# A rotary embedding kernel: the fp32 tail of the last row waits for another store and leaves in four DMAs

## The chip, the cores and the metric

The kernel runs on one core of a Trainium2 chip. The metric is the device time of one execution in microseconds (us), the median of several executions.

## The reference

The kernel computes an interleaved rotary position embedding on an fp32 tensor `x` of shape (8, 2048, 16, 64): batch, sequence, heads, head dimension. Neighbouring elements of the head dimension form a pair, which is rotated by an angle that depends on the position in the sequence and on the pair.

```
x1, x2 = x_pairs[..., 0], x_pairs[..., 1]
out1 = x1 * cos - x2 * sin
out2 = x1 * sin + x2 * cos
out = np.stack([out1, out2], axis=-1).reshape(batch, seq_len, num_heads, head_dim)
```

`cos` and `sin` have shape (2048, 32). The output is fp32 and as large as the input, 67.1 MB each.

## The kernel before, in words

The 2048 positions of a batch row are laid over 128 partitions, K = 16 positions to a partition, so a batch row is a tile of 128 x 16 x 1024 elements. In SBUF rows are held in bf16: `rows_sb` has NX = 5 slots of one batch row each, and row b lies in slot b % 5. Rows 5, 6 and 7 thus use the slots 0, 1 and 2 again.

Loads and stores of whole rows are DMAs that GpSimd (POOL) issues, and they convert between fp32 in HBM and bf16 in SBUF on the way (`load` at lines 51 to 56, `store` at lines 58 to 63; lines 56 and 63 move two rows in one DMA). Two pieces go in fp32 through a staging tile `st` instead, issued by SyncE (SP): the first HEAD = 4 positions of row 0, which ScalarE (ACT) then casts to bf16 (line 99), and the last TAIL = 4 positions of row 7, which ScalarE casts to fp32 (line 131) ahead of their store (line 132).

`rotate` (lines 79, 80 and 85) is three VectorE operations on a row in place: multiply by the signed sine table into `qt`, multiply by the cosine table, and add the pair-swapped `qt`.

The order is written out by hand. Rows 0 to 4 are loaded at the start, the stores of rows 0 and 1 are held back until the loads have landed (lines 111 and 112), and rows 5 to 7 are loaded once the slots are free. At the end the order on POOL is: the store of rows 3 and 4, of rows 5 and 6, and of the first twelve positions of row 7 (`store(7, k1=K - TAIL)`). Line 130 copies a single element of row 7 over an element of slot 4. Its result is used by nobody: as an instruction that writes to slot 4, it has to wait until the DMA that reads slot 4, the store of rows 3 and 4, has landed, and until row 7 is rotated. The cast at line 131 follows on the same engine, and the DMA at line 132 follows the cast. At line 158 the program ends: SP waits for all DMAs, the engines drain and meet.

Of the kernel before, what the change touches and what calls it, by code (L numbers as in the profile page):

```python
# [2 lines left out]

# [4 lines left out]


@with_exitstack  # L10
def kernel(
    ctx: ExitStack,
    tc: tile.TileContext,
    x: bass.AP,
    cos: bass.AP,
    sin: bass.AP,
    out: bass.AP,
):
    nc = tc.nc
    fp32 = mybir.dt.float32  # L20
    bf16 = mybir.dt.bfloat16
    mult = mybir.AluOpType.mult
    add = mybir.AluOpType.add

    B, S, H, D = x.shape
    P = 128
    K = S // P
    D2 = D // 2
    HD = H * D
    NX = 5  # L30
    HEAD = 4
    TAIL = 4
    REST = 2

    x_t = x.rearrange("b (p k) h d -> p b k (h d)", p=P, k=K)
    out_t = out.rearrange("b (p k) h d -> p b k (h d)", p=P, k=K)
    cos_t = cos.rearrange("(p k) c -> p (k c)", p=P, k=K)
    sin_t = sin.rearrange("(p k) c -> p (k c)", p=P, k=K)

    consts = ctx.enter_context(tc.tile_pool(name="consts", bufs=1))  # L40
    stage = ctx.enter_context(tc.tile_pool(name="stage", bufs=1))

    cos_sb = consts.tile([P, K * D2], fp32)
    sin_sb = consts.tile([P, K * D2], fp32)
    c_tab = consts.tile([P, K, D], bf16)
    s_tab = consts.tile([P, K, D], bf16)
    mark = consts.tile([1, 1], bf16)

    rows_sb = consts.tile([P, NX, K, HD], bf16)

    def load(b, n=1, k0=0, k1=K):
        s = b % NX
        if n == 1:
            nc.gpsimd.dma_start(out=rows_sb[:, s, k0:k1], in_=x_t[:, b, k0:k1])  # L54
        else:
            nc.gpsimd.dma_start(out=rows_sb[:, s : s + n], in_=x_t[:, b : b + n])  # L56

    def store(b, n=1, k1=K):
        s = b % NX
        if n == 1:  # L60
            nc.gpsimd.dma_start(out=out_t[:, b, :k1], in_=rows_sb[:, s, :k1])  # L61
        else:
            nc.gpsimd.dma_start(out=out_t[:, b : b + n], in_=rows_sb[:, s : s + n])  # L63

    def rotate(b, k0=0, k1=K):

        nk = k1 - k0
        xp = rows_sb[:, b % NX, k0:k1]
        qt = stage.tile([P, K, HD], bf16, name="qt", tag="work")

        def rows(a):
            return a.rearrange("p k (h e) -> p k h e", h=H, e=D)

        def tab(a):
            return dataclasses.replace(
                a, offset=a.offset + k0 * D, ap=[a.ap[0], [D, nk], [0, H], [1, D]]
            )

        nc.vector.tensor_tensor(out=rows(qt[:, :nk]), in0=rows(xp), in1=tab(s_tab), op=mult)  # L79
        nc.vector.tensor_tensor(out=rows(xp), in0=rows(xp), in1=tab(c_tab), op=mult)  # L80
        q_swap = dataclasses.replace(
            qt, offset=qt.offset + 1, ap=[qt.ap[0], [2, nk * HD // 2], [-1, 2]]
        )
        x3 = xp.rearrange("p k (a j) -> p (k a) j", j=2)
        nc.vector.tensor_tensor(out=x3, in0=x3, in1=q_swap, op=add)  # L85
        return qt

    with tc.manual_schedule():
        head = stage.tile([P, HEAD, HD], fp32, name="st", tag="work")
        nc.sync.dma_start(out=head, in_=x_t[:, 0, :HEAD])  # L90
        load(0, k0=HEAD)
        nc.gpsimd.dma_start(out=cos_sb, in_=cos_t)  # L92
        nc.gpsimd.dma_start(out=sin_sb, in_=sin_t)  # L93
        load(1, 2)
        load(3)
        load(4, k1=K - REST)
        load(4, k0=K - REST)

        nc.scalar.copy(out=rows_sb[:, 0, :HEAD], in_=head)  # L99
        s2 = s_tab.rearrange("p k (i j) -> p (k i) j", j=2)  # L100
        nc.vector.tensor_copy(out=s2[:, :, 0], in_=sin_sb)  # L101
        nc.vector.tensor_scalar_mul(s2[:, :, 1], sin_sb, -1.0)  # L102
        nc.vector.tensor_copy(  # L103
            out=c_tab.rearrange("p k (i j) -> p (k i) j", j=2),
            in_=cos_sb.to_broadcast([P, K * D2, 2]),
        )
        rotate(0, 0, HEAD)
        rotate(0, HEAD, K)
        rotate(1)

        nc.scalar.copy(out=mark, in_=rows_sb[:1, 4, K - REST - 1, :1])  # L111
        nc.scalar.copy(out=rows_sb[:1, 0, 0, :1], in_=rows_sb[:1, 0, 0, :1])  # L112
        store(0, 2)
        rotate(2)
        store(2)
        load(5, 2)
        load(7)
        rotate(3)
        rotate(4)
        store(3, 2)  # L120
        rotate(5)
        rotate(6)
        store(5, 2)
        rotate(7)
        store(7, k1=K - TAIL)


        tail = stage.tile([P, TAIL, HD], fp32, name="st", tag="work")
        last = rows_sb[:, 7 % NX]
        nc.scalar.copy(out=rows_sb[:1, 4, 0, :1], in_=last[:1, K - 1, :1])  # L130
        nc.scalar.copy(out=tail, in_=last[:, K - TAIL :])  # L131
        nc.sync.dma_start(out=out_t[:, B - 1, K - TAIL :], in_=tail)


# [1 line left out]
_INS = ['x', 'cos', 'sin']  # L136
_OUTS = [((8, 2048, 16, 64), 'float32')]


# [23 lines left out]
```

## Time and profile before

| | |
|---|---|
| median of 3 executions | 316.97 us (316.95 to 317.14) |
| the profiled execution | 317.52 us |
| its span in the profile | 315.7 us |
| VectorE busy | 210.3 us, 67% of the span |
| ScalarE, GpSimd busy | 8.9 us each, 3% |
| HBM read, written | 67.63 MB, 67.11 MB |

Times in the profile count from the start of the span. A line such as L132 is a line of the kernel. POOL is GpSimd, SP is SyncE, DVE is VectorE, ACT is ScalarE; a `q` behind a name is the sequencer of that engine. A DMA's time to landing runs from its issue to the semaphore that tells of its end. Each DMA engine of the core moves packets from two queues: q0 holds the DMAs that POOL issued, q1 those that SP issued. The profiled execution is one run, slightly longer than the median.

### The profile page before, as it was taken

How to read it: one execution, taken by the hardware profiler on the slowest of the kernel's cores; microseconds unless marked ns; L12 is line 12 of the kernel's file. 1: busy time of each engine (PE TensorE's matmuls, PEld its weight loads, DVE VectorE, ACT ScalarE, POOL GpSimd, SP SyncE). 2: the span in 40 equal slices, each digit the busy share in tenths (PEclk: the TensorE clock that was granted, in tenths of full speed). 3: DMA queues.
4: the chain of work that ended last, by engine and by line, in shares of the span. 5: the costliest groups of instructions: out<-in, count | busy, mean ns of one | idle time of the engine just before them, and what ended most of it. 6: DMA issues, size and time to landing. Idle time of an engine off the chain costs nothing.

```text
span 315.7 us, 117 instructions
## 1 busy us (share of the span) xinstructions
DVE 210.3 (67%) x30; ACT 8.9 (3%) x6; POOL 8.9 (3%) x18
## 2 busy tenths in 40 slices
DVE  0009995099999999999992000899999999900000
ACT  1030000000000000000000000000000000040000
POOL 5000000000000000000000000000000000000000
DMA  8999999999999999999999999999999999999997
GB/s 260 254 282 199 199 199 266 199 199 220 220 232 257 399 531 399 399 498 432 399 199 253 212 199 199 266 199 332 440 490 399 399 506 423 399 399 465 459 372 299
DMA packets 2816, 102.24 MB, mean 324 GB/s; under 512 B 256, under 2 KB 256, under 8 KB 512
## 3 DMA queue, kind: packets, MB, share of 16 engines
q0 software_dynamic: 2528, 98.04, 96.6%
q1 hardware_dynamic: 288, 4.19, 5.7%
HBM read 67.63 MB, written 67.11 MB: 427 GB/s over the span
## 4 chain that ended last, share of the span: by engine, by line
DVE 66%; another core or an unknown queue 13%; ACTq 1%; issue 0%; ACT 0%; DVEq 0%
DVE rows_sb L80 22%; DVE rows_sb L85 22%; DVE qt L79 22%; ACTq L158 1%; DVE c_tab L103 0%; ACT rows_sb L130 0%; DVEq L79 0%; DVEq L80 0%
## 5 line engine op out<-in xcount | busy, mean ns | idle before, releaser
L79 DVE TENSOR_TENSOR qt<-rows_sb,s_tab 128x16384 bf16<-128x16384 bf16 (+2 forms) x9 | 69.7, 7743 | 42.0 <-DMA rows_sb<-in_x_dram 41.8
L80 DVE TENSOR_TENSOR rows_sb<-rows_sb,c_tab 128x16384 bf16<-128x16384 bf16 (+2 forms) x9 | 69.7, 7743 | 0.4
L85 DVE TENSOR_TENSOR rows_sb<-rows_sb,qt 128x16384 bf16<-128x16384 bf16 (+2 forms) x9 | 69.7, 7744 | 0.3
L101 DVE CAST s_tab<-sin_sb 128x512 bf16<-128x512 f32 x1 | 0.5, 454 | 23.8 <-DMA sin_sb<-in_sin_dram 23.8
L63 POOL DMA_DIRECT2D out_dram<-rows_sb x3 | 2.2, 719 | 184.0 <-ACT rows_sb L112 94.3
L130 ACT COPY rows_sb<-rows_sb 1x1 bf16<-1x1 bf16 x1 | 0.2, 194 | 177.5 <-DVE rows_sb L85 177.5
L99 ACT CAST rows_sb<-st 128x4096 bf16<-128x4096 f32 x1 | 3.6, 3604 | 13.2 <-DMA st<-in_x_dram 13.2
L131 ACT CAST st<-rows_sb 128x4096 f32<-128x4096 bf16 x1 | 3.6, 3598 | 0.0
L54 POOL DMA_DIRECT2D rows_sb<-in_x_dram x5 | 2.9, 605 | 19.1 <-DMA out_dram<-rows_sb 18.3
L111 ACT COPY mark<-rows_sb 1x1 bf16<-1x1 bf16 x1 | 0.2, 193 | 80.3 <-DMA rows_sb<-in_x_dram 80.3
L61 POOL DMA_DIRECT2D out_dram<-rows_sb x2 | 1.1, 556 | 40.4 <-DVE rows_sb L85 40.4
L56 POOL DMA_DIRECT2D rows_sb<-in_x_dram x2 | 1.5, 728 | 25.0 <-DMA out_dram<-rows_sb 25.0
L99 ACT ACT_TABLE_LOAD x1 | 1.3, 1283 | 0.7 <-PEq L147 0.7
L103 DVE CAST c_tab<-cos_sb 128x1024 bf16<-128x1024 f32 x1 | 0.7, 685 | 0.0
L93 POOL DMA_DIRECT2D sin_sb<-in_sin_dram x1 | 0.6, 562 | 0.0
L92 POOL DMA_DIRECT2D cos_sb<-in_cos_dram x1 | 0.6, 554 | 0.0
L102 DVE TENSOR_SCALAR s_tab<-sin_sb 128x512 bf16<-128x512 f32 x1 | 0.4, 444 | 0.0
L112 ACT COPY rows_sb<-rows_sb 1x1 bf16<-1x1 bf16 x1 | 0.2, 188 | 0.0
L147 POOL MEMSET const-float32-0.0<- 128x1 f32 x1 | 0.1, 99 | 0.2 <-issue 0.2
L147 POOL MEMSET const-bfloat16-1.0<- 128x1 bf16 x1 | 0.1, 103 | 0.0
L147 POOL MEMSET const-float32-1.0<- 128x1 f32 x1 | 0.1, 99 | 0.0
L147 POOL MEMSET const-uint8-127<- 128x1 uint8 x1 | 0.1, 99 | 0.0
## 6 DMA issues: line engine op xcount, KB each, us to landing
rows_sb<-in_x_dram POOLq DMA_DIRECT2D x2, 8192.0 KB, 58.5
rows_sb<-in_x_dram POOLq DMA_DIRECT2D x2, 4096.0 KB, 68.0
out_dram<-rows_sb POOLq DMA_DIRECT2D x1, 6144.0 KB, 37.3
rows_sb<-in_x_dram POOLq DMA_DIRECT2D x1, 3584.0 KB, 94.8
rows_sb<-in_x_dram POOLq DMA_DIRECT2D x1, 3072.0 KB, 21.2
st<-in_x_dram SPq DMA_DIRECT2D x1, 2048.0 KB, 14.4
out_dram<-st SPq DMA_DIRECT2D x1, 2048.0 KB, 33.7
rows_sb<-in_x_dram POOLq DMA_DIRECT2D x1, 512.0 KB, 96.8
```

The source lines that it names most:

```text
L54: nc.gpsimd.dma_start(out=rows_sb[:, s, k0:k1], in_=x_t[:, b, k0:k1])
L56: nc.gpsimd.dma_start(out=rows_sb[:, s : s + n], in_=x_t[:, b : b + n])
L61: nc.gpsimd.dma_start(out=out_t[:, b, :k1], in_=rows_sb[:, s, :k1])
L63: nc.gpsimd.dma_start(out=out_t[:, b : b + n], in_=rows_sb[:, s : s + n])
L79: nc.vector.tensor_tensor(out=rows(qt[:, :nk]), in0=rows(xp), in1=tab(s_tab), op=mult)
L80: nc.vector.tensor_tensor(out=rows(xp), in0=rows(xp), in1=tab(c_tab), op=mult)
L85: nc.vector.tensor_tensor(out=x3, in0=x3, in1=q_swap, op=add)
L92: nc.gpsimd.dma_start(out=cos_sb, in_=cos_t)
L99: nc.scalar.copy(out=rows_sb[:, 0, :HEAD], in_=head)
L103: nc.vector.tensor_copy(out=c_tab.rearrange("p k (i j) -> p (k i) j", j=2), in_=cos_sb.to_broadcast([P, K * D2, 2]),)
L131: nc.scalar.copy(out=tail, in_=last[:, K - TAIL :])
L158: with _tile.TileContext(nc) as tc:
```

## The change

Line 130 writes its element to slot 6 % 5 = 1 instead of slot 4. Slot 1 is read by the store of rows 5 and 6. The tail, one DMA of four positions before, becomes four DMAs on SP: the first three positions of all 128 partitions, and the last position of partitions 0 to 111, 112 to 119 and 120 to 127.

```diff
         last = rows_sb[:, 7 % NX]
-        nc.scalar.copy(out=rows_sb[:1, 4, 0, :1], in_=last[:1, K - 1, :1])
+        nc.scalar.copy(out=rows_sb[:1, 6 % NX, 0, :1], in_=last[:1, K - 1, :1])
         nc.scalar.copy(out=tail, in_=last[:, K - TAIL :])
-        nc.sync.dma_start(out=out_t[:, B - 1, K - TAIL :], in_=tail)
+        nc.sync.dma_start(out=out_t[:, B - 1, K - TAIL : K - 1], in_=tail[:, : TAIL - 1])
+
+        for p0, p1 in ((0, P - 16), (P - 16, P - 8), (P - 8, P)):
+            nc.sync.dma_start(out=out_t[p0:p1, B - 1, K - 1], in_=tail[p0:p1, TAIL - 1])
```

## The prediction

> **What bounds the kernel now.** I read the page first: the shares of the engines, the strip of the DMA, the packets.
>
> ```profile
> span 315.7 us, 117 instructions
> DVE 210.3 (67%) x30; ACT 8.9 (3%) x6; POOL 8.9 (3%) x18
> DMA  8999999999999999999999999999999999999997
> DMA packets 2816, 102.24 MB, mean 324 GB/s; under 512 B 256, under 2 KB 256, under 8 KB 512
> q1 hardware_dynamic: 288, 4.19, 5.7%
> HBM read 67.63 MB, written 67.11 MB: 427 GB/s over the span
> ```
>
> VectorE, the busiest engine, works 67% of the span, while the DMA strip has a 9 in every slice but the first and the last. The 134.7 MB that cross HBM go at 427 GB/s over the whole span, the start and the end included. So the kernel is bound by its DMA engines, and an instruction matters only where it lets them run empty, or after their last byte. The packet row also shows how a DMA ends: the program issues 16 DMAs (9 loads and the head, 5 stores and the tail), and 256 packets are under 512 B, which is 16 for each. The row of q1 agrees: head and tail, 2 x 128 rows of 16 KB, are 256 packets, and 32 are left. So each of these DMAs is spread over 16 DMA engines and ends with a small packet on each.
>
> Then the timeline, for the stores and the end of the kernel.
>
> ```profile
> 99.68 0.72 POOL L63 DMA_DIRECT2D out_dram<-rows_sb  x1 [94.30 <-ACT rows_sb L112]
> 115.36 0.57 POOL L61 DMA_DIRECT2D out_dram<-rows_sb  x1 [14.96 <-DVE rows_sb L85]
> 250.95 0.72 POOL L63 DMA_DIRECT2D out_dram<-rows_sb  x1 [82.44 <-DVE rows_sb L85]
> 268.13 8.69 DVE L85 TENSOR_TENSOR rows_sb<-rows_sb,qt 128x16384 bf16<-128x16384 bf16 x1
> 276.86 0.19 ACT L130 COPY rows_sb<-rows_sb 1x1 bf16<-1x1 bf16 x1 [177.48 <-DVE rows_sb L85]
> 276.96 3.60 ACT L131 CAST st<-rows_sb 128x4096 f32<-128x4096 bf16 x1
> 277.13 0.54 POOL L61 DMA_DIRECT2D out_dram<-rows_sb  x1 [25.46 <-DVE rows_sb L85]
> 280.58 0.35 SPq L132 DMA_DIRECT2D out_dram<-st  x1
> ```
>
> The DMA view, asked for the stretch around each of these issues, gives the time from issue to landing; these are the answers for the issues at 99.68, 115.36, 250.95, 277.13 and 280.58.
>
> ```profile
> out_dram<-rows_sb POOLq DMA_DIRECT2D x1, 40.7
> out_dram<-rows_sb POOLq DMA_DIRECT2D x1, 44.3
> out_dram<-rows_sb POOLq DMA_DIRECT2D x1, 46.4
> out_dram<-rows_sb POOLq DMA_DIRECT2D x1, 6144.0 KB, 37.3
> out_dram<-st SPq DMA_DIRECT2D x1, 2048.0 KB, 33.7
> ```
>
> The landings are 99.68 + 40.7 = 140.38 (rows 0 and 1), 115.36 + 44.3 = 159.66 (row 2), 250.95 + 46.4 = 297.35 (rows 5 and 6), 277.13 + 37.3 = 314.43 (twelve positions of row 7) and 280.58 + 33.7 = 314.28 (the tail). Row 2 alone, 8.389 MB in fp32, landed 19.28 us after the store before it: 435 GB/s, which I take as the full rate. By its line, the wait on the store of rows 3 and 4 ended at 256.3:
>
> ```profile
> L130 ACTq EVENT_SEMAPHORE  x1: 38/38/38, 256.3 to 256.3; - x1
> ```
>
> From there to 314.43 the rows 5 and 6, row 7 and the tail go out, 24 MiB or 25.17 MB in 58.13 us, 433 GB/s. At 435.1 it would be 57.85 us: the whole end of the kernel has about 0.28 us to spare. VectorE finishes at 276.8 and the queue has 37.6 us of bytes left then.
>
> **The change part by part.** *The tie.* Line 130 now writes into slot 1, which the store of rows 5 and 6 still reads. ScalarE waits for that landing instead of for VectorE's last addition. Behind it in ScalarE's queue stands only the cast of the tail, and behind that SP's DMAs; POOL, whose last store is issued at 277.13, waits for none of them. With the tail no longer among its packets, rows 5 and 6 (16.78 MB at 435.1 GB/s, 38.56 us) land at 256.3 + 38.56 = 294.9. Copy and cast take 276.96 - 276.86 + 3.60 = 3.70 us, so SP issues at 298.6 instead of 280.58: 18 us later. What hides this is the rest of the store of row 7: 6.291 MB at 435.1 GB/s, 14.46 us from 294.9 on, to 309.3. SP's four issues at 0.35 us end at 300.0, over 9 us before the queue would run empty. The bytes are the same 8.389 MB behind 294.9, and at 435.1 GB/s they end at 314.2, or at 314.4 with the same slack as now. Cost 0. Only the order changes: row 7 first, the tail last and alone. If this cover were gone, the price would be the gap itself, microsecond for microsecond.
>
> *Three more DMAs on one queue.* Each adds its ending packets behind its bytes. The nearest rows are two small loads, one right behind the other, in POOL's queue:
>
> ```profile
> 1.93 0.55 POOL L92 DMA_DIRECT2D cos_sb<-in_cos_dram  x1
> 2.47 0.56 POOL L93 DMA_DIRECT2D sin_sb<-in_sin_dram  x1
> cos_sb<-in_cos_dram POOLq DMA_DIRECT2D x1, 256.0 KB, 21.2
> sin_sb<-in_sin_dram POOLq DMA_DIRECT2D x1, 256.0 KB, 21.3
> ```
>
> They land at 23.13 and 23.77, 0.64 us apart; 262,144 bytes at 435.1 GB/s are 0.60, so the second DMA cost 0.04 us beyond its bytes, although its pieces are small. Stores may cost more: the 0.28 us of slack in the last 58.13 us holds three changes from one DMA to the next, 0.09 each if all of it is theirs. Bounds 3 x 0.04 = 0.12 and 3 x 0.09 = 0.27 us; I take +0.2, nearer to the stores.
>
> The Trainium skill speaks against this part. Its page "DMA: Bandwidth & Descriptors" gives a DMA about 2.0 us fixed on top of its bytes (section on the anatomy of one DMA), and its rules for kernel authors say of transfers to separate groups of partitions that one transfer over all 128 is the better form. If the three new DMAs paid that in series, an estimate from this page would be +6 us; the 0.04 us above disagrees for DMAs that stand queued behind one another.
>
> *How the last position is spread.* One row of it is 4 KB. A DMA engine moves 435.1 / 16 = 27.2 GB/s, so a row is 0.15 us. Now each engine carries 8 of 128 rows. Split as 112, 8 and 8, some engines can get 9 and others 7. Which engines end last matters, and the windows at the very end show how far apart they are (columns: share of the DMA engines, then GB/s; with 0 GB/s only ending packets start there):
>
> ```profile
> 313.40:313.50 0.10, 0.00 (x0) 0.00 (x0) 0.00 (x0) 1.00 0.20 0
> 313.50:313.60 0.10, 0.00 (x0) 0.00 (x0) 0.00 (x0) 1.00 0.14 0
> 313.60:313.70 0.10, 0.00 (x0) 0.00 (x0) 0.00 (x0) 1.00 0.03 0
> 313.70:313.80 0.10, 0.00 (x0) 0.00 (x0) 0.00 (x0) 1.00 0.06 0
> 313.80:313.90 0.10, 0.00 (x0) 0.00 (x0) 0.00 (x0) 1.00 0.03 0
> ```
>
> Most engines end before 313.6, a few up to 0.3 to 0.4 us later. Taking a row from the late ones and giving it to others can win 0.4 us at most; giving more rows to a late one costs 0.15 for one row, 0.3 for two. The view doesn't name the engines, so I take 0 and keep both ends, -0.4 and +0.3.
>
> The same page of the Trainium skill, in its section on why a DMA counts to 16, says that the number of DMA engines is the largest up to 16 that divides the slowest dimension, and for SP the lowest-numbered ones: then 112 rows go 7 to an engine, and 8 rows go to the first 8 engines, twice. The 9 and 7 above would follow; no run here shows it yet.
>
> *Behind the last byte.* Line 158 is where the program ends:
>
> ```profile
> L158 SPq EVENT_SEMAPHORE  x8: 17/28/28, 297.3 to 315.7; - x8
> L158 POOLq EVENT_SEMAPHORE  x4: 17/17/17, 315.1 to 315.6; - x4
> L158 POOLq DRAIN  x3: 45/82/37927, 277.1 to 315.5; - x3
> L158 SPq DRAIN  x3: 7/7/7, 314.7 to 315.3; - x3
> ```
>
> POOL's drain begins at 277.1 and lasts 37.93 us, so it ends at 315.0, 0.6 us behind the landing of POOL's last store at 314.43, and POOL's next semaphore instruction follows at 315.1. SP is through its waits by 314.7. If the drain ends with POOL's own DMAs, it will be over early, since row 7 now ends several us before the tail, and SP is what is late: 0.3 us are won. If it ends for another reason, 0. I take -0.3. SP's list grows by three completions; from 314.43 to 314.7 it stepped through five of the eight semaphore instructions in 0.3 us, so three more are at most +0.2; as waits already passed cost nothing behind the last landing, I take 0.
>
> The sum is 0 + 0.2 + 0 - 0.3 + 0 = -0.1 us. The profiled execution took 317.52 us, 1.8 us of it outside the span of 315.7, which the change doesn't touch; it would become 317.4. It stands 0.55 us above the median of 316.97, so in the median I expect 316.9 us. The ends of all terms give 0.12 - 0.4 - 0.3 = -0.6 and 0.27 + 0.3 + 0.2 = +0.8: 316.4 to 317.7.
>
> **The rivals.** *The end is cut shorter (faster).* The late DMA engines are among those that lose rows (-0.4), POOL's drain is off the path (-0.3), the slack of 0.28 us that may come from mixing two queues goes too, and the completions cost 0.12: together -0.86, 316.1 us. For it speaks that all three lie behind or at the last bytes, where nothing hides a gain; against it, that each must come out at its best end.
>
> *The four DMAs of the tail run one after the other (slower).* With row 7 gone, only SP's queue has work, and a gap between its DMAs has no cover. If each new DMA begins its bytes only when the one before has landed, it pays a start each time. The first DMA of the kernel shows one: issued at 0.74, its bytes are moving in the second of these windows, so at most 1.3 us.
>
> ```profile
> 0.74 0.37 SPq L90 DMA_DIRECT2D st<-in_x_dram  x1
> 0.00:1.00 1.00, 0.00 (x0) 0.26 (x1) 0.20 (x4) 1.00 0.00 0
> 1.00:2.00 1.00, 0.00 (x0) 1.00 (x1) 0.75 (x2) 1.00 0.96 213
> ```
>
> Three starts of up to 1.3 us make +3.9, 320.9 us. It decides as soon as one gap is over 0.25 us. For it: no row shows two DMAs of SP's queue back to back. Against it: the 0.64 us between cos and sin. A milder form, in which each ending holds its queue for 0.3 to 0.5 us, gives +0.7 to +1.3 with the drain's gain off: 317.7 to 318.3.
>
> *The DMAs of 8 rows are not spread (slower).* If both went to one DMA engine, it would carry 7 + 16 = 23 rows instead of 8, 15 x 0.15 = +2.3 us, 319.2 us. Against it: all 16 DMAs of the kernel ended on 16 engines; but none of them had so few rows.
>
> *The change does not do what it says.* If the tie held back nothing, the tail would mix with rows 5 and 6 as now and the time would not move; at 276.86 that store had 20.5 us to go, so the tie must bind. It is counted with no change.
>
> **How the numbers follow.** About 0.2%, 0.63 us, is what a measurement of this kernel can tell from no change: from 316.3 to 317.6 is the same. My forecast, 316.9, has 0.60 and its own range lies almost wholly in there. The shorter end has 0.20. The slower cases have 0.20: 0.07 for the full series, 0.07 for its milder form, 0.06 for rows that are not spread. The range 316.2 to 318.2 leaves out the full series and the unspread rows (0.13) and about 0.06 at the lower end and above.
>
> **What would show it.** Right: ScalarE's copy at line 130 waits for the store of rows 5 and 6 and runs near 295; SP's four issues lie between 298 and 301; row 7 lands about 3 to 4 us before the tail; POOL's drain ends before SP's; everything up to 276.8 is unchanged. Wrong: a stretch between 310 and 314 in which the DMA share falls clearly below 1 (the queue is stopped between DMAs), a last DMA that lands over 1 us behind the third (not spread), an issue of the tail later than 309, or a drain of POOL that still ends last.

## The result and the profile after

The changed kernel takes 316.56 us (316.33 to 317.32, 22 runs), the kernel before on the same chips 316.98 us. The ratio is 0.9988, 95% interval 0.9982 to 0.9993: a gain of 0.4 us, inside the 0.2% that the prediction called the same, and clear of zero over this many runs.

The page of the changed kernel, the rows that answer to those of before:

```profile
span 314.7 us, 122 instructions
DMA packets 2976, 102.24 MB, mean 325 GB/s; under 512 B 288, under 2 KB 288, under 8 KB 672
q1 hardware_dynamic: 448, 4.19, 3.4%
```

The span is 1.0 us shorter, but not all of it is the change. The store of row 7 is issued at 276.56 here and at 277.13 before, 0.57 us earlier, although nothing ahead of it was changed; over all profiled runs of this study it lies between 276.43 and 277.22. So I read everything from that issue on. The DMA queues stand equally far along at it: in all thirteen profiles the store of rows 3 and 4 landed 20.9 us earlier. To the end of the span it is 38.57 us before and 38.14 us after, 0.43 less, which is what the medians say.

The timeline of its end:

```profile
276.56 0.55 POOL L61 DMA_DIRECT2D out_dram<-rows_sb  x1 [25.46 <-DVE rows_sb L85]
294.36 0.19 ACT L130 COPY rows_sb<-rows_sb 1x1 bf16<-1x1 bf16 x1 [195.43 <-DMA out_dram<-rows_sb]
298.08 0.36 SPq L132 DMA_DIRECT2D out_dram<-st  x1
298.49 1.18 SPq L135 DMA_DIRECT2D out_dram<-st  x3
```

The DMA view's times to landing for the stores issued at 250.38 (rows 5 and 6), at 276.56, at 298.08 and, of the 112 partitions, at 298.49:

```profile
out_dram<-rows_sb POOLq DMA_DIRECT2D x1, 43.9
out_dram<-rows_sb POOLq DMA_DIRECT2D x1, 6144.0 KB, 33.6
out_dram<-st SPq DMA_DIRECT2D x1, 1536.0 KB, 14.3
out_dram<-st SPq DMA_DIRECT2D x1, 448.0 KB, 15.0
```

ScalarE's copy now waits for the DMA and runs at 294.36. Row 7 lands at 276.56 + 33.6 = 310.16, the three positions at 312.4, the 112 partitions at 313.5: the tail is last. For the two DMAs of 8 rows the view has no time; by the semaphore events of the trace the last of them lands at 313.84. That is 37.28 us behind the issue of row 7, and in the kernel before the last landing, by the same events at 314.41 (314.43 from the view's tenths), is 37.28 us behind it as well. The end of the program, at line 161 now:

```profile
L161 SPq EVENT_SEMAPHORE  x9: 17/28/10432, 299.7 to 314.6; - x9
L161 POOLq EVENT_SEMAPHORE  x4: 17/17/17, 314.0 to 314.6; - x4
L161 POOLq DRAIN  x3: 45/93/34222, 276.5 to 314.4; - x3
L161 SPq DRAIN  x3: 7/7/7, 313.9 to 314.2; - x3
```

POOL's long drain ends at 276.5 + 34.2 = 310.7, 0.6 us behind the landing of row 7, and is off the path. SP's drain comes at 313.9 and POOL's first semaphore instruction, at which the engines meet, at 314.0. Counted from the issue of row 7, engines met at 37.9 to 38.0 us before and at 37.4 us after. SP's drain moved less, from 37.6 to 37.3. In this pair of profiles the bytes end no earlier, and the gain lies behind the last of them.

### The profile page after: what moved, and what is told of

Its sections match the earlier page's. It is cut to its first block, busy times and chain, and to the rows that moved or that the text cites. A ratio compares the mean times of both kernels' runs of the same rounds, so it can differ in the third digit from the quotient of the medians.

```text
span 314.7 us, 122 instructions
## 1 busy us (share of the span) xinstructions
DVE 210.4 (67%) x30; ACT 8.9 (3%) x6; POOL 8.9 (3%) x18
## 4 chain that ended last, share of the span: by engine, by line
DVE 42%; issue 17%; DMA 14%; another core or an unknown queue 13%; ACTq 1%; POOL 0%; ACT 0%; DVEq 0%; POOLq 0%
DMA out_dram<-rows_sb 14%; DVE rows_sb L80 14%; DVE rows_sb L85 14%; DVE qt L79 14%; ACTq L161 1%; POOL out_dram L63 0%; DVE c_tab L103 0%; ACT rows_sb L130 0%; ACTq L130 0%; DVEq L80 0%; DVEq L79 0%; POOLq L63 0%; POOLq L61 0%
## 6 DMA issues: line engine op xcount, KB each, us to landing
out_dram<-rows_sb POOLq DMA_DIRECT2D x1, 6144.0 KB, 33.6
```

## The experiments

The theories were: D, the gain is POOL's drain; B, it is the spread of the last position over the DMA engines; M, it is that the two queues no longer mix. The last column of the table is the time from the issue of row 7 to the meeting of the engines, from the profile of each kernel (38.0 for the kernel before).

| kernel | median us | ratio to before (95%) | issue to meeting |
|---|---|---|---|
| the change | 316.56 | 0.9988 (0.9982 to 0.9993) | 37.4 |
| e1 tie alone | 316.19 | 0.9974 (0.9963 to 0.9984) | 37.2 |
| e2 split alone | 316.72 | 0.9991 (0.9983 to 1.0) | 37.6 |
| e3 tie, two DMAs | 316.26 | 0.9976 (0.9967 to 0.9985) | 37.3 |
| e4 tie, even split | 316.48 | 0.9982 (0.9973 to 0.999) | 37.3 |
| e5 tie, tail from POOL | 316.83 | 0.9998 (0.9989 to 1.0007) | 37.8 |
| e6 tie, nine DMAs | 317.39 | 1.0013 (1.0004 to 1.0022) | 38.4 |
| e7 tie to row 7 | 321.47 | 1.0142 (1.0128 to 1.0156) | 42.5 |
| e8 tie, later cast | 316.34 | 0.9979 (0.9971 to 0.9988) | 37.2 |
| e9 tie, seven DMAs | 316.61 | 0.9989 (0.9979 to 0.9998) | 37.5 |

### The two halves of the change

e1, the tie alone (the edit against the changed kernel):

```diff
-        nc.sync.dma_start(out=out_t[:, B - 1, K - TAIL : K - 1], in_=tail[:, : TAIL - 1])
-
-        for p0, p1 in ((0, P - 16), (P - 16, P - 8), (P - 8, P)):
-            nc.sync.dma_start(out=out_t[p0:p1, B - 1, K - 1], in_=tail[p0:p1, TAIL - 1])
+        nc.sync.dma_start(out=out_t[:, B - 1, K - TAIL :], in_=tail)
```

> The tie alone: ScalarE's copy goes to slot 1, the tail stays one DMA of four positions. Theory D (the gain is POOL's drain, which ends 0.6 us behind the landing of POOL's last store and no longer sets the end once SP's tail lands last): row 7 lands about 310, POOL's drain ends near 311, and the gain over the kernel before is all of the change's 0.4 us or more, 0.4 to 0.6 us, since no further DMAs are to be ended. Theory B (the gain is the spread of the last position, 9 rows on some DMA engines and 7 on others): no gain, within 0.1 us of the kernel before. Theory M (the gain is the 0.28 us that mixing the two queues cost): 0.2 to 0.3 us of gain, seen as an earlier last landing and not behind it.

It gained 0.80 us, 0.26%: more than the change, and more than D alone had put on it. Its timeline:

```profile
276.49 0.54 POOL L61 DMA_DIRECT2D out_dram<-rows_sb  x1 [25.46 <-DVE rows_sb L85]
298.04 0.35 SPq L132 DMA_DIRECT2D out_dram<-st  x1
```

The tail's time to landing in its DMA view:

```profile
out_dram<-st SPq DMA_DIRECT2D x1, 2048.0 KB, 15.5
```

And the line at which it ends:

```profile
L158 POOLq EVENT_SEMAPHORE  x4: 17/17/17, 313.7 to 314.3; - x4
L158 POOLq DRAIN  x3: 45/82/34677, 276.5 to 314.1; - x3
L158 SPq DRAIN  x3: 7/7/7, 313.6 to 313.9; - x3
```

The last landing is 298.04 + 15.5 = 313.54, and the engines meet 0.2 us later, at 313.7; before it was 314.43 and 315.1, 0.6 to 0.7 us. That is about 0.5 us of the 0.8. The other 0.25 is an earlier last landing, 37.05 us behind the issue of row 7 against 37.30. An earlier last landing, by 0.2 to 0.3 us, is also what M expected here, so M may hold for this smaller part. B is out: a gain with no uneven spread.

e2, the split alone (against the changed kernel):

```diff
-        nc.scalar.copy(out=rows_sb[:1, 6 % NX, 0, :1], in_=last[:1, K - 1, :1])
+        nc.scalar.copy(out=rows_sb[:1, 4, 0, :1], in_=last[:1, K - 1, :1])
```

> The split alone: ScalarE's copy stays on slot 4, so that the tail is issued near 280.6 as before, but in four DMAs. Theory B: the whole gain of the change, 0.4 us. Theory M: no gain, as the queues mix as before. Theory D: it depends on which queue ends last; the tail's small pieces take their turns more slowly than the pieces of row 7, so some rows should be left over when POOL's queue is empty, over 0.6 us of them (about 8 of 16 pieces of 4 KB at 0.15 us make 1.2 us), and then POOL's drain is off the path and the gain is 0.3 to 0.5 us without any tie.

The issue of row 7 in its timeline:

```profile
277.15 0.54 POOL L61 DMA_DIRECT2D out_dram<-rows_sb  x1 [25.46 <-DVE rows_sb L85]
```

Its time to landing:

```profile
out_dram<-rows_sb POOLq DMA_DIRECT2D x1, 6144.0 KB, 36.6
```

The last line of the program:

```profile
L161 POOLq EVENT_SEMAPHORE  x4: 17/17/17, 314.7 to 315.3; - x4
L161 POOLq DRAIN  x3: 45/93/37235, 277.1 to 315.1; - x3
L161 SPq DRAIN  x3: 7/7/7, 314.6 to 314.9; - x3
```

Without a tie, row 7 lands at 277.15 + 36.6 = 313.75 and POOL's drain is over at 314.3, ahead of SP's at 314.6, as D expected. The gain by the medians is 0.27 us, just under the lower end of the forecast, with an interval that reaches 1.0. So the two halves win the same thing, and do not add up: 0.80 and 0.27 alone, 0.42 together.

### What the split costs

e3 has the last position in one DMA, `((0, P),)`, e4 has it as `((0, P - 32), (P - 32, P - 16), (P - 16, P))`, both with the tie.

> The change with the last position as one DMA of 128 partitions: the tail is two DMAs, 8 rows of the last position on each DMA engine, two DMA endings fewer than in the change. Theory D: as fast as the change or faster, 0.4 to 0.6 us below the kernel before, the difference to the change being the two endings at 0.04 to 0.1 us each and one row of 4 KB, 0.15 us, on the engines that carried 9. Theory B: slower than the change by what the uneven spread brought, back near the kernel before.

> The change with the last position as 96, 16 and 16 partitions instead of 112, 8 and 8: as many DMAs, but 6 + 1 + 1 = 8 rows on every DMA engine. Theory D: no loss against the change, rather 0.1 us faster, as no engine has 9 rows. Theory B: the gain of the change is gone or at least 0.15 us smaller.

Both are at least as fast as the change, e3 by 0.30 us. e4, with as many DMAs as the change but eight rows everywhere, is 0.08 below its first 22 runs and level with its second measurement (e10, below): 9 and 7 rows against 8 and 8 can't be told apart. That leaves the number of DMAs: e4 has two more than e3 with the same even spread and takes 0.22 us more, though the intervals of the two overlap.

e6 and e9 put a price on one ending. e6 has the last position in eight DMAs of 16 partitions, e9 in six (e9 against the changed kernel):

```diff
-        for p0, p1 in ((0, P - 16), (P - 16, P - 8), (P - 8, P)):
+        for p0, p1 in ((0, 48), (48, 64), (64, 80), (80, 96), (96, 112), (112, P)):
```

> The tie, with the last position in eight DMAs of 16 partitions: one row on each DMA engine and one ending on each, so the spread stays even and there are seven endings more than with the last position in one DMA (316.26 us). If an ending costs 0.04 us of its queue, 0.3 us more; at 0.1 us, 0.7 us more (316.5 to 317.0). If the DMAs of one queue had to start anew each time, over 3 us more.

> The tie, with the last position in six DMAs (48 partitions and five times 16), eight rows on every DMA engine as in the kernel with the last position in one DMA (316.26 us), and five endings more, all of whose DMAs SP can issue without waiting for an earlier landing. If an ending costs 0.04 us, as the prediction's lower row had it, 0.2 us more (316.46); at 0.07, the value it took, 0.35 more (316.6); at 0.1, 0.5 more (316.75). A fresh start each time would give 317.5 or more.

e6 took 1.13 us more than e3, above the forecast, and it did not measure what it was made for. Among SP's waits stands this:

```profile
SPq L135 <- DMA out_dram<-st: 10.7, 1, 10.7
```

The source line of the eight DMAs, with their first and last start and their times to landing:

```profile
L135 SPq DMA_DIRECT2D out_dram<-st x8: 315/420/432, 298.5 to 312.4; - x8
DMA to landing us min/median/max: 1.9/13.2/14.2
```

SP waited 10.7 us for a landing before it could issue the last of them at 312.4. By the packets in the trace, the last bytes of the DMAs ahead of it started at 313.0 and its own first at 313.25, so it ran alone; it needed 1.9 us from issue to landing for 64 KB. e9 stays below that number of DMAs: five endings more than e3 cost 316.61 - 316.26 = 0.35 us, 0.07 each. The intervals of e3 and e9 overlap, so this is a rough price. The trace of e9 has a second one:

```profile
L135 SPq DMA_DIRECT2D out_dram<-st x6: 419/420/432, 298.6 to 300.9; - x6
DMA to landing us min/median/max: 13.0/13.7/14.4
```

The first of the six, 48 partitions, lands at 298.6 + 14.4 = 313.0 and the last at 300.9 + 13.0 = 313.9; by the semaphore events it is 312.98 and 313.94. The five DMAs of 16 partitions thus land 0.19 us apart. Their 64 KB are 0.15 us at the prediction's 435.1 GB/s, which leaves 0.04 us for each.

e10 and e11 are the change and the tie alone once more, side by side on one chip.

> The changed kernel once more, on the same chip as the tie alone, for their difference: 316.5 to 316.6 by the runs so far.

> The tie alone once more, beside the changed kernel: 316.2, 0.3 to 0.4 us below it, if three endings and one more row on some DMA engines are what the split costs; as slow as the changed kernel if the difference between their first runs was one between chips.

They took 316.49 us (0.9981, 0.9972 to 0.999) and 316.25 us (0.9973, 0.9962 to 0.9985), 0.24 apart; three endings at 0.04 to 0.07 make 0.12 to 0.21. The intervals against the kernel before overlap; that the tie alone is faster rests on two pairs of medians (0.37 and 0.24 us) and on the profiles (37.4 against 37.2).

### The drain, by itself

e5 leaves the tie and the bytes of e1 and lets POOL issue the tail (against e1):

```diff
-        nc.sync.dma_start(out=out_t[:, B - 1, K - TAIL :], in_=tail)
+        nc.gpsimd.dma_start(out=out_t[:, B - 1, K - TAIL :], in_=tail)
```

> The tie alone, with the tail's one DMA issued by POOL instead of SP, so that POOL's own queue lands last. The bytes, the tie and the order are those of the kernel with the tie alone (316.19 us). Theory D (POOL's drain ends about 0.6 us behind the landing of its last DMA): the drain is back on the path, POOL's semaphore instruction follows the last landing by 0.6 to 0.7 us instead of 0.17, and the time is 0.4 to 0.6 us above the tie alone, near 316.7. A rival (the gain comes from the order of the bytes and from no longer mixing two queues, theory M): no loss against the tie alone, 316.0 to 316.2.

The timeline of e5:

```profile
276.43 0.55 POOL L61 DMA_DIRECT2D out_dram<-rows_sb  x1 [25.46 <-DVE rows_sb L85]
298.22 0.54 POOL L132 DMA_DIRECT2D out_dram<-st  x1 [21.25 <-ACT st L131]
```

The tail's time to landing:

```profile
out_dram<-st POOLq DMA_DIRECT2D x1, 2048.0 KB, 15.3
```

Its last line:

```profile
L158 POOLq EVENT_SEMAPHORE  x4: 17/17/17, 314.2 to 314.8; - x4
L158 POOLq DRAIN  x3: 45/88/15947, 298.2 to 314.6; - x3
L158 SPq DRAIN  x3: 7/7/7, 313.7 to 314.4; - x3
```

The tail lands at 298.22 + 15.3 = 313.52, as in e1. SP is through at 313.7, but POOL's drain lasts until 298.2 + 15.9 = 314.1 and the engines meet at 314.2. Against e1 the time is 0.64 us longer and no longer to be told from the kernel before. So D is shown for the part behind the last byte: same bytes, same tie, the same last landing, and only whose DMA lands last differs.

### The cover of the tie

e7 ties to the store of row 7 itself (the edit below, against e1), e8 keeps the tie of e1 and casts the tail twice:

```diff
-        nc.scalar.copy(out=rows_sb[:1, 6 % NX, 0, :1], in_=last[:1, K - 1, :1])
+        nc.scalar.copy(out=rows_sb[:1, 7 % NX, 0, :1], in_=last[:1, K - 1, :1])
```

> The tie alone, but to the store of row 7: ScalarE's copy writes slot 2, so the cast and the tail's DMA come only when the DMA queue is empty. By the cover theory of the prediction (the 18 us of delay are free because the store of row 7 fills the queue) the gap now shows in full: copy and cast 3.7 us, SP's issue and the start of the bytes 1.3 to 1.7 us, semaphore steps 0.4 us; 5.3 to 6.0 us above the tie alone, 321.5 to 322.2 us. If the queue were not what sets the end, much less.

> The tie alone, with the cast of the tail done twice, so that its DMA is issued 3.6 us later, still some 7 us before the queue would run empty; fewer of the tail's pieces mix with those of row 7. Theory D and the cover: the same as the tie alone, 316.1 to 316.3. Theory M (mixing costs): up to 0.15 us less. If the start of the tail is late against the emptying queue, more than 316.4.

The timeline of e7:

```profile
276.62 0.55 POOL L61 DMA_DIRECT2D out_dram<-rows_sb  x1 [25.46 <-DVE rows_sb L85]
308.90 0.19 ACT L130 COPY rows_sb<-rows_sb 1x1 bf16<-1x1 bf16 x1 [209.91 <-DMA out_dram<-rows_sb]
312.62 0.34 SPq L132 DMA_DIRECT2D out_dram<-st  x1
```

Two of its windows (the last two columns are the share of the DMA engines and GB/s):

```profile
309.00:313.00 4.00, 0.00 (x0) 3.60 (x2) 0.00 (x0) 1.00 0.00 0
313.00:314.00 1.00, 0.00 (x0) 0.00 (x0) 0.00 (x0) 1.00 0.62 262
```

For 4 us no byte moves, and the time is 5.28 us above e1, at the lower end of the forecast. The same 3.7 us of copy and cast cost nothing in e1. In e8 the timeline has the tail's issue here:

```profile
276.55 0.54 POOL L61 DMA_DIRECT2D out_dram<-rows_sb  x1 [25.46 <-DVE rows_sb L85]
301.67 0.34 SPq L133 DMA_DIRECT2D out_dram<-st  x1
```

and the DMA view its time to landing:

```profile
out_dram<-st SPq DMA_DIRECT2D x1, 2048.0 KB, 11.9
```

It lands at 313.57, 37.0 us behind the issue of row 7, as in e1, where it was issued 3.6 us earlier. So 3.6 us more of delay are still covered. Mixing the queues for a shorter time brings nothing that these runs can show; but M expected at most 0.15 us here, which is less than the interval of e8, so this neither supports M nor rules it out.

## Why the prediction was right, point by point

**The bound and the cover** held. The copy was forecast at 294.9 and SP's issue at 298.6; they came at 294.36 and 298.08, and from the issue of row 7 that is 17.8 and 21.5 us, as forecast to 0.1. The tie cost nothing where the queue was full, and its uncovered price is e7's 5.28 us. Row 7 landed 3.7 us ahead of the last landing, as forecast.

**The endings** held: 0.07 us each by the medians of e9 and e3, the value behind the forecast's +0.2 for three, and 0.04 by e9's landings, its lower bound.

**The spread** was left at 0 between -0.4 and +0.3, and e4 finds nothing over 0.1. How the rows are spread is now seen: q1 has 448 packets, which is 144 for the head, 144 for the three positions, 112 + 16, and twice 8 + 8. So each DMA of 8 rows used 8 DMA engines, as the Trainium skill's page "DMA: Bandwidth & Descriptors" has it (section on why a DMA counts to 16); the rival with unspread rows is out. Which engines those were, and which end last, was not settled.

**Behind the last byte** is the step that was mis-sized. The mechanism was right: POOL's drain ended the kernel, and left the path. The forecast took 0.3 us, the distance from POOL's drain at 315.0 to SP's at 314.7, as if SP needed 0.3 us behind the landing as before. But SP had stepped through its other waits while the tail was still moving. In e1 its drain follows the landing by under 0.1 us, so the whole way from landing to meeting shrank from 0.6 or 0.7 us to 0.2: a term of -0.5, not -0.3. With it the sum is 0 + 0.2 - 0.5 = -0.3 of the measured -0.4 us. The rest is a term that the prediction had at 0: with the tie alone the last landing comes 0.25 us earlier. In the change it is about what the three further DMAs take back, so that the last landing stays at 37.28 us.

The forecast of 316.9 us was thus 0.3 us too slow, by two terms that erred the same way, the drain by 0.2 us and the last landing by 0.25 us. The measured time lies in the stated range because that range was wide, from -0.8 to +1.2 us about the time before.

**The rivals.** The shorter end was half right: its price of 316.1 us is nearly met by e1, 316.19, which has the drain off and the last landing 0.25 us earlier and pays for no endings. The rival's slack of 0.28 us has the size of that earlier landing.

The DMAs in series did not happen: the landings at 313.5 and 313.84 leave no room for them. The sign that the prediction named, a fall of the DMA share, can't be read in stretches this short. These are two windows of the changed kernel and one of the kernel before:

```profile
311.00:311.70 0.70, 0.00 (x0) 0.00 (x0) 0.00 (x0) 1.00 0.82 351
311.70:312.20 0.50, 0.00 (x0) 0.00 (x0) 0.00 (x0) 1.00 0.81 328
306.00:307.00 1.00, 0.00 (x0) 0.00 (x0) 0.00 (x0) 1.00 9.12 786
```

A share of 9.12 shows that the view books a packet's whole time where the packet starts, so 0.82 and 0.81 show no stop. The milder form's own terms give +0.6 to +1.2 us, not the +0.7 to +1.3 of the prediction.

The last DMA of e6, which ran alone, took 1.9 us to its landing; DMAs queued behind one another pay 0.04 to 0.07. The Trainium skill's page "DMA: Bandwidth & Descriptors" gives a DMA that GpSimd issues about 2.0 us besides its bytes (section on the anatomy of one DMA). The first figure here, of a DMA that SP issued, is near that; the price of a queued one is far below it. So the rule against splitting that the prediction weighed holds in its sign, since the split makes the kernel slower than the tie alone by 0.2 to 0.4 us, and not in its size.

What stays open is the earlier last landing of the tie alone. e5, with all in POOL's queue, has it too (313.52 - 276.43 = 37.09 us against 37.30), so it does not need SP's queue. It fits M, since e5 mixes no queues at all, but it would fit any other effect that the tie has on the order of the bytes, and no run separated them.

## What to carry to other kernels

Where a kernel is bound by DMA to its end, look at which queue lands last: in this kernel a last store by POOL left 0.6 us of POOL's drain behind it, while a last store by SP let that drain and SP's earlier waits pass under its bytes. To reorder the end, a delay was free as long as other stores filled the queue for longer than the delay (e1 and e8), and cost its full length where they did not (e7). Do not split a queued DMA without a reason that is worth more than the 0.04 to 0.07 us that each piece cost here.

## What was not expected of the hardware

POOL's drain ended 0.6 to 0.7 us behind the landing of the last DMA that POOL had issued; by the semaphore events it is 0.62 to 0.66 us in all thirteen profiles. And with nine DMAs from SP behind the head's, SP itself stopped for 10.7 us before it issued the last one. The trace of e6 shows on what: that DMA counts up the same semaphore as the tail's first DMA, and SP waited until the first had landed. So it is the program that used a semaphore twice, and no run here shows a limit of the chip.
